# Squared deviation from the row mean: small leading loads folded into two large loads on one DMA queue

## The chip, the cores and the metric

The kernel runs on one core of one Trainium2 chip. The metric is the device time in microseconds (us); lower is better. The six executions of the kernel before agree within 0.16% (82.86 to 82.99 us). All differences in this study are below 3%, most below 0.5%, so they are read only against runs of the kernel before on the same chip.

A word used throughout: a *packet* is one contiguous run that one of the core's 16 DMA engines moves. Here it is one partition's part of one transfer, so a transfer over 128 partitions gives each engine 8 packets. The trace records the start, duration and size of each packet; where I quote these, the figures stand in plain fences or in the text, because the views of the profile only show them summed up. The record of a packet does not name its engine. I sorted the packets into 16 lines by letting each start where another had ended; for the large packets this is clear, for the small ones only sums and means over all 16 engines are safe.

## The reference

```python
batch, dim = 1024, 4096            # x: float32, axis = -1
mean = np.mean(x, axis=axis, keepdims=True)
return ((x - mean) ** 2).astype(np.float32)
```

16.78 MB are read and 16.78 MB written; there is next to no arithmetic per byte.

## The kernel before

Each of two tiles holds 4 rows on each of 128 partitions, so one partition's part of a tile is 64 KiB, contiguous in memory. Both tiles stay in on-chip memory, and all loads are issued at the start:

```python
for i in range(ntiles):                       # ntiles = 2, Q = 4, D = 4096, HEAD = 512
    x_tile = io.tile([P, Q * D], F32)
    if i == 0:
        nc.sync.dma_start(out=x_tile[:, :HEAD], in_=x_t[i][:, :HEAD])
        nc.sync.dma_start(out=x_tile[:, HEAD:], in_=x_t[i][:, HEAD:])
    else:
        end = Q * D - HEAD
        nc.scalar.dma_start(out=x_tile[:, end:], in_=x_t[i][:, end:])
        nc.sync.dma_start(out=x_tile[:, :end], in_=x_t[i][:, :end])
    ...
```

Per row, VectorE sums it (`pairs`, `neg_mean`) and ScalarE squares with the negative mean as bias. The last eighth of the last row is squared on VectorE. After its four rows a tile is stored in one transfer of 64 KiB runs from SP's queue.

## Time and profile before

| | before |
|---|---|
| median time | 82.99 us (82.96 to 82.99, 3 runs) |
| span in the profile | 81.4 us |
| DMA queues, share of 16 engines' span | 95.0% + 1.1% |
| VectorE, ScalarE busy | 26%, 36% |
| first packet starts, last packet ends | 1.75 us, 80.23 us |

The DMA engines work from 1.75 to 80.23 us, first loads, then stores, with no pause but 0.10 us on average at the turn between the two; compute lies beneath. The end is set by the engine that finishes last (80.23 us, and 1.13 more to the end of the span). The lines that show this are in the prediction. One more, in the windows cut at the stage borders, shows the start (the last two columns are DMA share and GB/s; a packet is credited to the window in which it starts, hence shares over 1):

```profile
1.70:4.10 2.40, 0.00 (x0) 0.00 (x0) 0.00 (x0) 1.00 1.76 642
```

In this window lie the 256 small packets of 2 KiB and the first large packet of each engine.

### The profile page before, as it was taken

The page shows a single profiled execution, that of the slowest core. Times are in us where ns is not written, and L with a number is a line of the kernel's source. Part 1 is how long each engine was busy: PE and PEld are TensorE (multiplying, and loading weights), DVE is VectorE, ACT ScalarE, POOL GpSimd, SP SyncE. Part 2 cuts the span into 40 slices and gives each one's busy share as a digit, 9 for nine tenths or more (in the row PEclk, how much of TensorE's full clock was granted, in tenths as well). Part 3 has the DMA queues.
Part 4 walks back from the last instruction along what each step waited for, and adds up shares of the span by engine and source line. Part 5 has one row for each costly group of instructions (what it writes and reads, how often), then busy time and mean ns, then how long its engine had stood idle before and what let it go on. Part 6 is the DMA issues. An engine that isn't in the chain of part 4 may idle for free.

```text
span 81.4 us, 87 instructions
## 1 busy us (share of the span) xinstructions
DVE 20.8 (26%) x20; ACT 29.4 (36%) x9; POOL 0.2 (0%) x4
## 2 busy tenths in 40 slices
DVE  0000000000059999600039999700000000000000
ACT  0000000000054999999502999999600000000000
POOL 0000000000000000000000000000000000000000
DMA  1974999999759999995799993899996599999390
GB/s 22 704 343 187 499 499 499 499 499 437 343 218 499 499 499 499 499 406 250 343 516 515 515 515 161 354 515 515 515 516 290 258 483 515 515 515 419 161 451 0
DMA packets 864, 33.55 MB, mean 412 GB/s; under 512 B 96, under 2 KB 96, under 8 KB 352
## 3 DMA queue, kind: packets, MB, share of 16 engines
q1 hardware_dynamic: 720, 33.29, 95.0%
q10 hardware_dynamic: 144, 0.26, 1.1%
HBM read 16.78 MB, written 16.78 MB: 412 GB/s over the span
## 4 chain that ended last, share of the span: by engine, by line
DMA 49%; ACT 13%; ACTq 4%; DVE 3%; SPq 1%; issue 0%
DMA x_tile<-in_x_dram 49%; ACT x_tile L77 13%; ACTq L119 4%; DVE pairs L66 3%; SPq L53 1%; SPq L52 0%; DVE neg_mean L66 0%
## 5 line engine op out<-in xcount | busy, mean ns | idle before, releaser
L77 ACT ACTIVATE x_tile<-x_tile,neg_mean 128x4096 f32<-128x4096 f32 (+1 forms) x8 | 28.2, 3590 | 5.7 <-DVE neg_mean L66 5.7
L66 DVE CUSTOM_DVE_ANT_0 pairs<-x_tile 128x2048 f32<-128x2048 f32 x8 | 18.3, 2292 | 31.6 <-DMA x_tile<-in_x_dram 31.4
L77 ACT ACT_TABLE_LOAD x1 | 1.3, 1283 | 23.2 <-DMA x_tile<-in_x_dram 23.2
L87 DVE TENSOR_TENSOR x_tile<-x_tile 128x512 f32<-128x512 f32 x2 | 1.4, 692 | 0.1
L86 DVE TENSOR_SCALAR x_tile<-x_tile,neg_mean 128x512 f32<-128x512 f32 x2 | 1.0, 488 | 0.1
L66 DVE DVE_READ_ACCUMULATOR2_ANT neg_mean<- 128x1 f32 x8 | 0.7, 82 | 0.0
L105 POOL MEMSET const-bfloat16-1.0<- 128x1 bf16 x1 | 0.1, 102 | 0.0
L105 POOL MEMSET const-uint8-127<- 128x1 uint8 x1 | 0.1, 102 | 0.0
L105 POOL MEMSET const-float32-0.0<- 128x1 f32 x1 | 0.1, 99 | 0.2 <-issue 0.2
L105 POOL MEMSET const-float32-1.0<- 128x1 f32 x1 | 0.1, 99 | 0.0
## 6 DMA issues: line engine op xcount, KB each, us to landing
x_tile<-in_x_dram SPq DMA_DIRECT2D x2, 7936.0 KB, 31.1
x_tile<-in_x_dram ACTq DMA_DIRECT2D x1, 256.0 KB, 3.8
x_tile<-in_x_dram SPq DMA_DIRECT2D x1, 256.0 KB, 3.6
out_dram<-x_tile SPq DMA_DIRECT2D x2, 21.9
```

Of the source, the lines that this page charges most:

```text
L53: nc.sync.dma_start(out=x_tile[:, HEAD:], in_=x_t[i][:, HEAD:])
L66: inorder(nc.vector.tensor_tensor_reduce(out=pairs, in0=row[:, :HALF], in1=row[:, HALF:], scale=-inv_d, scalar=0.0, op0=ADD, op1=ADD, accu ...
L77: nc.scalar.activation(out=row[:, :cut], in_=row[:, :cut], func=ACT.Square, bias=neg_mean, scale=1.0,)
L86: nc.vector.tensor_scalar_add(out=rest, in0=rest, scalar1=neg_mean)
L87: nc.vector.tensor_mul(out=rest, in0=rest, in1=rest)
L105: nc = _bacc.Bacc("TRN2", target_bir_lowering=False, num_devices=1)
L119: with _tile.TileContext(nc) as tc:
```

## The change

The intent: no small packets, no second queue, the longest runs throughout. Two loads and two stores, all with 64 KiB runs, all on SP's queue. Compute is untouched.

```diff
-    HEAD = 512
...
-        if i == 0:
-            nc.sync.dma_start(out=x_tile[:, :HEAD], in_=x_t[i][:, :HEAD])
-            nc.sync.dma_start(out=x_tile[:, HEAD:], in_=x_t[i][:, HEAD:])
-        else:
-            end = Q * D - HEAD
-            nc.scalar.dma_start(out=x_tile[:, end:], in_=x_t[i][:, end:])
-            nc.sync.dma_start(out=x_tile[:, :end], in_=x_t[i][:, :end])
+        nc.sync.dma_start(out=x_tile, in_=x_t[i])
```

## The prediction

The forecast's sum comes to 1.95 + 0.25 + 77.28 + 0.1 = 79.6 us for the last end, a gain of about 0.6, and 82.99 - 0.6 = 82.4 us. That run length is no lever rests on the two lengths shown, both at 434 GB/s.

> **What bounds the kernel now.** I read the page first, from its strip of 40 slices and its queue part.
>
> ```profile
> span 81.4 us, 87 instructions
> DMA  1974999999759999995799993899996599999390
> DMA packets 864, 33.55 MB, mean 412 GB/s; under 512 B 96, under 2 KB 96, under 8 KB 352
> q1 hardware_dynamic: 720, 33.29, 95.0%
> q10 hardware_dynamic: 144, 0.26, 1.1%
> ```
>
> The two queues together keep the 16 DMA engines busy for 95.0 + 1.1 = 96.1% of the span, while the page gives VectorE 26% and ScalarE 36%. The dips in the strip (4, 5, 3) are no idle time: a slice is 2.03 us and one large packet lasts longer than that, so a slice is credited with a packet or not. The windows cut at stage borders show it: from 4.1 to 22.8 us the DMA share is 1.00.
>
> ```profile
> 0.00:1.70 1.70, 0.00 (x0) 0.00 (x0) 0.20 (x4) 1.00 0.00 0
> 4.10:22.80 18.70, 0.00 (x0) 0.00 (x0) 0.00 (x0) 1.00 1.00 435
> 80.20:81.40 1.20, 0.00 (x0) 0.00 (x0) 0.00 (x0) 1.00 0.00 0
> ```
>
> The last two columns are DMA share and GB/s. Nothing moves before 1.7 us or after 80.2. The chain of waits, next, looks as if compute mattered:
>
> ```profile
> 1.64 40.26 DMA x_tile<-in_x_dram
> 41.92 2.29 DVE pairs L66
> 51.56 3.60 ACTq L119
> 55.16 3.17 ACT x_tile L77
> ```
>
> It stops at 55.16 + 3.17 = 58.33 us, when the last store is only being issued; the store that follows, some 22 us of it, is not in it. So I don't take its shares. The timeline and the table of DMA issues put the true order together:
>
> ```profile
> 0.73 0.39 ACTq L56 DMA_DIRECT2D x_tile<-in_x_dram  x1
> 0.73 0.38 SPq L52 DMA_DIRECT2D x_tile<-in_x_dram  x1
> 1.16 0.42 SPq L53 DMA_DIRECT2D x_tile<-in_x_dram  x1
> 23.29 2.29 DVE L66 CUSTOM_DVE_ANT_0 pairs<-x_tile 128x2048 f32<-128x2048 f32 x1 [23.29 <-DMA x_tile<-in_x_dram]
> 39.73 18.97 SPq L88 DMA_DIRECT2D out_dram<-x_tile  x2
> out_dram<-x_tile SPq DMA_DIRECT2D x2, 21.9
> ```
>
> The first store is issued at 39.73, the second at about 58.4. The packet records of the trace give the rest. One packet is one partition's run, and an engine carries 8 partitions of each transfer. A load packet of 63,488 B takes 2.342 us, with the next one starting 2.339 us after it; a store packet of 65,536 B takes 2.418 us, at a pitch of 2.415. The loads of tile 1 finish at 40.9 to 41.5 us and the store's packets start at 40.93 to 41.50 on the same engines, with a gap on two engines only (0.28 and 0.29 us). Store 0 then runs into store 1 without a hole, as store 1 is issued at 58.4 and store 0's last packets end at 60.2 to 60.9. Thus a DMA engine's line is unbroken from its first packet to its last, and compute lies under it. The kernel's time is: lead 1.75, small packets until the first large load packet (3.47 to 4.07, by engine), 16 load packets x 2.339 = 37.4, 16 store packets x 2.415 = 38.6, end at 79.57 to 80.23, and 1.13 of closing to 81.37. The measured 82.99 is 1.62 over that span; I take that as a constant.
>
> [...]16 x 65,536 B / 2.415 us = 434 GB/s for the stores and 16 x 63,488 B / 2.339 us = 434 for the loads, so [...]run length is no lever on the large packets. [...]the small packets of the ACT queue run from 1.92 to 4.07 us in between those of SP's (1.75 to 3.90), and the first large packet on an engine waits for both. [...]the two small loads are 256 KiB each, [...]16 small packets per engine cost 1.87 us where the bytes at the large packets' rate are 16 x 2,048 B / (65,536 B / 2.415 us) = 1.21.[...]
>
> **The change, part by part.** Removed: the two small loads (2 x 128 packets of 2 KiB, 2 x 16 completion packets), one issue on SP and one on ACT. The 4 KiB per partition go into the two large loads, whose packets grow from 63,488 to 65,536 B. Compute, stores and buffers stay; in the order of instructions nothing moves on VectorE or ScalarE.
>
> Bytes first: they are the same, so the 1.21 us per engine just computed stays. It comes back as 16 load packets x (2.415 - 2.339) = 1.21. What can go is the excess of the small packets, 1.87 - 1.21 = 0.66 us per engine. It has two parts. Of the 256 small packets 223 take 85 ns on average, 9 more than 2,048 B at the full rate (76): 16 x 9 = 0.15 us per engine. The other 33, about two per engine, are slow, 332 ns on average, 0.25 over the rest: 2 x 0.25 = 0.5 us per engine. They are mostly the first of their queue on an engine, so I read them as a start-up cost. The 0.15 goes for certain. Of the 0.5, one start-up may remain, because the first 64 KiB packet of an engine is now the first packet of all: 0.25. Sum: gain 0.66 at most, 0.41 with one start-up kept.
>
> Second, the spread. The engine that ends last sets the time. Before, the small packets scatter the first large ones over 0.60 us, and the last end (80.23) lies 0.3 after the mean end (79.92, mean of the 16). The first packets themselves started within about 0.2 us. If the engines now start within 0.2 and stay so, the last lies about 0.1 to 0.15 after the mean: gain about 0.15 to 0.2.
>
> The other way, added up: first packets at 1.75 to 1.95, one start-up of 0.25, 32 x 2.415 = 77.28, 0.1 at the turn from load to store, gives a last end of about 79.6, against 80.23: gain 0.65. Both ways agree on 0.5 to 0.8; I take 0.6. Time: 82.99 - 0.6 = 82.4 us, ratio 0.993.
>
> What is hidden: tile 0 is whole after 8 packets instead of the small ones and 8, so its landing moves from 23.2 to about 1.95 + 0.25 + 8 x 2.415 + 0.5 (last packet to VectorE, as before: 22.78 to 23.29) = 22.0. The compute of a tile takes 39.73 - 23.29 = 16.4 us, so store 0 is issued at about 38.4 rather than 39.73. Loads keep the engines until about 40.9, so those 1.3 us buy only the two short gaps at the turn. The ACT issue of 0.39 us is at a time when ScalarE waits for data until 23.24: worth nothing. Tile 1 lands at about 41.3, its compute ends at about 57.8, before store 0 is through at about 60.3.
>
> **The rivals.** *Start-up cost moves over whole:* the first 64 KiB packets each pay what the small ones paid, 0.5 us. For it: the slow packets may be slow because they are first at the memory, not because they are small.[...] Then 82.99 - 0.15 - 0.1 = 82.7. *Loads in step run slower:* all engines now read at nearly the same offset of rows 128 KiB apart, where before they were up to 0.6 us apart. If load packets took 5% longer, 38.6 x 0.05 = 1.9 us: 84.3 us, within 2%, just. Against it: two lanes of before that start within 0.001 us of each other show the same 2.342 us as all others, and the stores in the same layout run at 434 GB/s. *The early landing counts:* whoever trusts the chain of waits takes the 1.3 us off the end: 81.7. Against it: the engines have no hole to close. *A hole at the turn:* if compute were later than reckoned, store 0 would start late; the margin is about 2.5 us between issue and the end of the loads, and before it was 1.2 and already nearly enough.
>
> **Range and chances.** The floor is 32 x 2.415 = 77.28 plus lead 1.75, closing 1.13 and 1.62 outside the span: 81.8. Two per cent faster is 81.33, below this floor, so "faster" needs packets quicker than any seen: 0.02. "Slower" needs over 84.65, a load slowdown of over 5%: 0.03. The middle is 82.4; the floor plus some spread gives 82.0 as the low end, the moved start-up and a little loss gives 82.9 as the high end.
>
> **What would show it right or wrong.** Right: 576 packets on one queue (4 x 128 + 4 x 16), none between 512 B and 8 KB; load packets at 2.415 us; first packets at 1.75 to 1.95; VectorE starts at about 22.0, store 0 is issued at about 38.4, and no hole in the DMA line; last end about 79.6, span about 80.8. Wrong: a load packet over 2.45 us on average (the step that run length is no lever), a first packet longer by more than 0.5 us or a later first packet (start-up), a spread of last ends over 0.6 us, or VectorE's earlier start carried through to the end.

## The result and the profile after

The changed kernel took 83.32 us (median of 6 runs, 83.25 to 83.38) against 82.97 us before (6 runs, 82.86 to 82.99). The ratio is 1.0047, 95% interval 1.0034 to 1.0059: within 2%, but slower, where 82.4 had been forecast. Ratios here are the mean time of one kernel's fast runs over that of the other's fast runs of the same rounds, so they are not quite the ratio of the medians quoted.

The page of the changed kernel, first its strip and queue lines:

```profile
span 81.5 us, 81 instructions
DMA  9299975999984999987899998399998689999830
DMA packets 576, 33.55 MB, mean 412 GB/s; under 512 B 64, under 2 KB 64, under 8 KB 64
q1 hardware_dynamic: 576, 33.55, 95.8%
```

There are 576 packets on one queue, and the only ones under 8 KB are 64 of 4 B, 16 for each of the four transfers, which the prediction calls completion packets (96 before, for six transfers). But the engines are busy for 95.8% of the span, hardly less than the 96.1% of before, though 352 - 64 = 288 small packets are gone. So something else takes their time. The windows, same cuts as before:

```profile
1.70:4.10 2.40, 0.00 (x0) 0.00 (x0) 0.00 (x0) 1.00 1.30 437
4.10:22.80 18.70, 0.00 (x0) 0.00 (x0) 0.00 (x0) 1.00 1.04 449
80.20:81.40 1.20, 0.00 (x0) 0.00 (x0) 0.00 (x0) 1.00 0.00 0
```

The first window shows it. Its 437 GB/s over 2.4 us is one packet of 64 KiB per engine, 16 x 65,536 B / 2.4 us. At the full rate such packets take 16 x 2.418 us = 38.7 us of engine time, which is 38.7 / (16 x 2.4) = 1.01 of the window. The view has 1.30. The first packets take 1.3 times as long as they should. (The second window holds 128 packet starts, 8 rounds, hence a share a little over 1.) The packet records, sorted by start, say so one by one:

```
changed kernel, first 64 KiB packet of each engine (steady duration: 2.418 us)
start us  1.74 1.74 1.76 1.76 1.77 1.80 1.81 1.85 1.86 1.89 1.91 1.98 2.00 2.32 2.34 2.38
took us   3.11 2.96 3.21 3.05 3.07 3.16 3.12 3.09 3.45 3.11 3.10 3.35 3.54 2.57 2.98 2.93
```

On average a first packet takes 3.11 us, which is 0.69 over the steady duration. The other 496 packets of the kernel, loads and stores, are clean: none takes over 2.44 us. In the kernel before no large packet was over 2.364 us at the start, and the small ones had carried an excess of 0.66 us per engine.

Now the ends. A DMA engine's end is its first start, its first packet, and 31 packets at a pitch of 2.415 us:

| mean or extreme over the 16 engines, us | before | after |
|---|---|---|
| mean last end | 79.96 | 79.91 |
| latest last end | 80.23 | 80.39 |
| latest minus mean | 0.28 | 0.48 |
| span | 81.37 | 81.54 |

For after, the mean is 1.93 + 3.11 + 31 x 2.415 = 79.91, as recorded. The latest engine started at 2.00 and took 3.536 for its first packet: 2.00 + 3.54 + 74.87 = 80.41, recorded 80.39. So on average the engines end only 0.04 us sooner than before, and the last of them ends 0.16 us later, because the start-up is now paid in one lump per engine that varies from 0.15 to 1.12 us.

The small gain of the mean does not come from the start: the loads end at 41.27 us on average, 0.15 later than before (41.12), and on the last engine at 41.75, 0.25 later (41.50). It comes from behind them. The 0.10 us at the turn is gone, as store 0 was issued earlier, and the stores ran at 2.415 us per packet rather than 2.421, 0.10 over 16 packets. The pause before had a good side: it was paid mostly by the engines that were early, so it cut the distance from mean to last from 0.38 to 0.28.
The spans differ by 0.17. The two profiled executions took 83.14 and 83.32 us, a difference of 0.18; the other 0.17 of the 0.35 between the medians is that the profiled execution of before was slower than its median. No profile of a faster one was at hand.

The timeline after answers to the lines shown of before:

```profile
0.73 0.86 SPq L48 DMA_DIRECT2D x_tile<-in_x_dram  x2
22.81 2.29 DVE L57 CUSTOM_DVE_ANT_0 pairs<-x_tile 128x2048 f32<-128x2048 f32 x1 [22.81 <-DMA x_tile<-in_x_dram]
39.25 19.66 SPq L79 DMA_DIRECT2D out_dram<-x_tile  x2
out_dram<-x_tile SPq DMA_DIRECT2D x2, 22.2
```

VectorE starts at 22.81 rather than 23.29, store 0 is issued at 39.25 rather than 39.73, and little comes of it: the engines had only the 0.10 us at the turn to close, and the store waits in the queue a little longer. (The last line is from the table of DMA issues.)

### The profile page after: what moved, and what is told of

Read it like the earlier page. It is cut to its first block, busy times and chain, and to the rows that moved or that the text cites. A ratio compares the mean times of both kernels' runs of the same rounds, so it can differ in the third digit from the quotient of the medians.

```text
span 81.5 us, 81 instructions
## 1 busy us (share of the span) xinstructions
DVE 20.8 (25%) x20; ACT 29.4 (36%) x9; POOL 0.2 (0%) x4
## 3 DMA queue, kind: packets, MB, share of 16 engines
q1 hardware_dynamic: 576, 33.55, 95.8%
## 4 chain that ended last, share of the span: by engine, by line
DMA 50%; ACT 13%; ACTq 4%; DVE 3%; SPq 0%; issue 0%
DMA x_tile<-in_x_dram 50%; ACT x_tile L68 13%; ACTq L110 4%; DVE pairs L57 3%; SPq L48 0%; DVE neg_mean L57 0%
```

## The experiments

Three theories were put against each other at first. *A:* each DMA engine pays about 0.6 to 0.7 us once at its start, in whatever packets come first, and the scatter of this decides the end. *B:* large packets at the start cost more than small ones do. *C:* the issue of the second load, from about 1.2 to 1.6 us, disturbs the first packets. "Excess" below is what packets took over the steady duration of their size in the same trace, summed per engine and averaged over 16 engines. Diffs are against the changed kernel unless said otherwise. The costs per byte and per packet in the expectations are estimates from the traces of the two kernels: 27.1 B per ns is 65,536 B / 2.418 us, and 0.009 us per packet is what a packet of 2 KiB took over its bytes at that rate (85 against 76 ns).

### e1_head: the small head load alone

```diff
+        if i == 0:
+            nc.sync.dma_start(out=x_tile[:, :512], in_=x_t[i][:, :512])
+            nc.sync.dma_start(out=x_tile[:, 512:], in_=x_t[i][:, 512:])
+        else:
+            nc.sync.dma_start(out=x_tile, in_=x_t[i])
```

> The small head load of tile 0 (512 columns, SP) is put back, the ACT tail load is not. Theory A (start-up: each DMA engine pays about 0.6 us once at its start, in whatever packet comes first; the end is set by how far this start scatters the engines): the 8 small packets carry the start-up, their sum is about 1.2 us per engine, no large packet is over 2.45 us, mean last end about 79.8 to 79.9 us; the time lies between the two kernels, 82.9 to 83.2, by the scatter. Theory B (a large first packet pays more at start than small ones do, so small packets in front are a gain in themselves): large packets all at 2.42, time at or below the kernel before, 82.6 to 82.9. Theory C (issuing the second large load disturbs the first packets): second large load is issued at the same time as before, so first large packets would stay clean; no forecast of its own.

83.55 us (7 runs, 83.19 to 84.50) against 83.10; ratio of fast runs 1.0045 (1.0023 to 1.0066). The expectation of clean large packets failed: the small packets had an excess of 0.22 us, and the first large ones had 0.38 more. The sum, 0.60, fits theory A: eight packets of 2 KiB discharge a part of the start-up, not all of it. The profiled execution was a slow one (84.50 us: two engines had load packets of 3.0 and 3.3 us at 39.4 and 39.6 us), so its ends are not compared. Theory B is not borne out: a small load in front was no gain.

### e2_tail: the small ACT load alone

```diff
+        if i == 0:
+            nc.sync.dma_start(out=x_tile, in_=x_t[i])
+        else:
+            end = Q * D - 512
+            nc.scalar.dma_start(out=x_tile[:, end:], in_=x_t[i][:, end:])
+            nc.sync.dma_start(out=x_tile[:, :end], in_=x_t[i][:, :end])
```

> The ACT tail load of tile 1 (last 512 columns) is put back, the head load is not; the first packet on SP's queue is a 64 KiB one. Theory A: on each engine either the small ACT packet or the 64 KiB packet comes first; the first 64 KiB packet takes 2.6 to 3.5 us again, the time is that of the changed kernel, 83.2 to 83.4. Theory B: the same, 83.2 to 83.5, as the large packet is still the first on SP's queue, with 8 small ACT packets in between costing up to 0.15 us more. If it is instead the second queue that made the kernel before quick, the time is 82.9 to 83.0.

83.30 us against 83.10, ratio 1.0030 (1.0018 to 1.0042). On every engine a 64 KiB packet came first, with an excess of 0.67 us on average; the first small ACT packet started only at 4.76 us. As expected by A and B. A second queue that came behind a large packet changed nothing here.

### e3_warm: a tiny throw-away load in front

```diff
+        if i == 0:
+            warm = scratch.tile([P, 128], F32)
+            nc.sync.dma_start(out=warm, in_=x_t[i][:, :128])
         nc.sync.dma_start(out=x_tile, in_=x_t[i])
```

> The changed kernel with a throw-away load of 128 columns (512 B per partition, 64 KiB in all) into a spare tile ahead of the two 64 KiB-run loads. Pure additional bytes cost 8 x 512 B / 27.1 B per ns = 0.15 us per engine. Theory A: the 8 tiny packets carry the start-up, the 64 KiB packets are all 2.418 us, the mean last end moves by 0 to +0.2 against the changed kernel (79.9 to 80.1), time 83.2 to 83.5 unless the scatter shrinks. Theory B: the large packets no longer pay their large start-up, time falls to 82.7 to 83.1 although more bytes move. A third outcome, first 64 KiB packet still over 2.6 us, would say that the start-up belongs to large packets and not to an engine's first work.

84.06 us against 83.10, ratio 1.0120 (1.0105 to 1.0135): worse than any outcome listed. The third outcome came: the 512 B packets took about 27 ns each and showed no start-up, and the first large packets still had an excess of 0.47 us. On top, the engines had run out of tiny packets at 2.1 us, while the large load, issued 0.42 us later than in the changed kernel, brought first packets only at 2.24 to 3.12 us. Fourteen load packets around the issue of store 0 (39.50 us) took 2.48 to 3.00 us as well, 0.18 us per engine.

```profile
0.72 0.38 SPq L50 DMA_DIRECT2D warm<-in_x_dram  x1
1.15 0.90 SPq L51 DMA_DIRECT2D x_tile<-in_x_dram  x2
```

So eight packets of 512 B per engine in front did not clear the start-up.

### e4_late2: the second load issued late

```diff
+        if i == 1:
+            nc.vector.memset(x_tile[:, :2 * D], 0.0)
         nc.sync.dma_start(out=x_tile, in_=x_t[i])
```

> The changed kernel with the second load held back some 9 us by a VectorE memset of half of its tile[...]. It is issued well before the first load ends, so the DMA line stays whole. Theory C[...]: first packets fall to about 2.5 us and start within 0.2 us, last end about 79.5, time 82.7 to 83.0. Theories A and B: first packets 2.6 to 3.5 us as in the changed kernel, time 83.2 to 83.4.

83.38 us against 83.10, ratio 1.0039 (1.0021 to 1.0057). The second load was issued at about 9.3 us, long after the first packets were through, and the excess was 0.75 us, latest end 0.53 us after the mean. One load packet, at 39.2 us, took 2.62. Theory C falls.

### e5_hole: a second start from standing

```diff
+        if i == 1:
+            nc.vector.memset(x_tile, 0.0)
+            nc.vector.memset(x_tile, 0.0)
         nc.sync.dma_start(out=x_tile, in_=x_t[i])
```

> The changed kernel with the second load held back to about 30 us by two VectorE memsets of its whole tile, so that the DMA engines stand idle from about 22 to 31 us and start a second time (compute of tile 0 is late too; the time, about 92 us, is of no interest). If the start-up is paid whenever engines that stand idle start together, the first packet of the second load takes 2.6 to 3.5 us like that of the first, some 0.7 us over 2.418 on average. If it is paid once in an execution (first touch of the memory or of the queue), the second load's first packets take 2.42 us.

The windows of this run, cut at the first start, the hole, the second start and the steady part (columns: stretch, length, busy time and count of VectorE, ScalarE and GpSimd, clock, DMA share, GB/s):

```profile
1.70:4.70 3.00, 0.49 (x1) 0.00 (x0) 0.00 (x0) 1.00 1.02 350
22.60:36.00 13.40, 13.40 (x2) 1.24 (x1) 0.00 (x0) 1.00 0.00 0
36.00:39.00 3.00, 2.96 (x3) 1.70 (x1) 0.00 (x0) 1.00 1.06 350
39.50:50.00 10.50, 5.88 (x8) 10.50 (x4) 0.00 (x0) 1.00 1.01 437
```

The engines stood from 22.6 to 36 us. In the first 3 us after each start they moved one packet each (350 GB/s x 3 us / 16 = 65.6 KB) at a share of 1.02 and 1.06, where 2.418 / 3 = 0.81 would do. The packet records: 3.06 us on average at the first start, 3.18 at the second (2.72 to 3.45). The start-up is paid at every start from standing, not once in an execution. Each engine's last load packet was slow too, by 1.03 us on average; see e7.

### e6_pitch: another layout of rows

```diff
-    x_t = x.rearrange("(p n q) d -> n p (q d)", p=P, q=Q)
-    out_t = out.rearrange("(p n q) d -> n p (q d)", p=P, q=Q)
+    x_t = x.rearrange("(n p q) d -> n p (q d)", p=P, q=Q)
+    out_t = out.rearrange("(n p q) d -> n p (q d)", p=P, q=Q)
```

> The changed kernel with rows given to partitions tile by tile, so that a tile's 64 KiB runs follow one another in memory without gaps (pitch of 64 KiB rather than 128). If the start-up comes from the 16 engines meeting in the same places of memory at the start, it changes with the pitch: first packets 2.42 to 2.7, or far over 3.5. If not, first packets 2.6 to 3.5, extra of about 0.7 us per engine, time 83.2 to 83.5 as in the changed kernel.

83.35 us against 83.16, ratio 1.0025 (1.0010 to 1.0040). First packets 2.75 to 3.71 us, excess 0.75. In this second layout the start-up is the same, so the rival of engines reading "in step" finds no support at the start either. Five load packets at 38.7 to 39.3 us took 2.50 to 2.62; store 0 was issued at 39.17.

### e7_32k: loads cut in two

```diff
+        half = Q * D // 2
+        nc.sync.dma_start(out=x_tile[:, :half], in_=x_t[i][:, :half])
+        nc.sync.dma_start(out=x_tile[:, half:], in_=x_t[i][:, half:])
```

> The changed kernel with each load cut in two of 32 KiB runs: twice the load packets. Theory A (start-up is a time per engine, not a share of the packet): the first packet takes its 1.21 us plus about 0.67 on average, not plus 0.35; the per-packet cost adds 16 x 0.009 = 0.15 us; mean last end 79.9 to 80.2, time 83.2 to 83.6. If the start-up is in proportion to the first packet's size, the extra is about 0.35 and the time 82.8 to 83.1.

The start went by theory A: the first packets of 32 KiB took 1.81 us on average, 0.59 over their steady 1.213 (0.61 with a few slow second packets), nearly as much in time as the 64 KiB packets had. But the time was 84.40 us against 83.16, ratio 1.0153 (1.0136 to 1.0170), 0.8 above the forecast. The loss sits elsewhere: each engine's last two load packets, from 38.6 us on, took 1.79 us instead of 1.21, together 1.14 us per engine. The timeline shows what was new at that time:

```profile
31.95 20.77 SPq L81 DMA_DIRECT2D out_dram<-x_tile  x2
```

As compute could start on the first half of tile 0, store 0 was issued at 31.95 us, some 9.3 us before the loads would have ended (41.2 us, their mean end less the 1.14). That led to e10 and e14.

### e8_sp4: the four loads of before, all on SP's queue

```diff
-        nc.sync.dma_start(out=x_tile, in_=x_t[i])
         tiles.append(x_tile)
+    end = Q * D - 512
+    nc.sync.dma_start(out=tiles[0][:, :512], in_=x_t[0][:, :512])
+    nc.sync.dma_start(out=tiles[1][:, end:], in_=x_t[1][:, end:])
+    nc.sync.dma_start(out=tiles[0][:, 512:], in_=x_t[0][:, 512:])
+    nc.sync.dma_start(out=tiles[1][:, :end], in_=x_t[1][:, :end])
```

> All four loads of the kernel before, but on SP's queue alone, both small ones first: 16 small packets per engine ahead of the large ones, one queue. If 16 small packets (some 1.9 us in which the start-up is spread over many packets[...]) is what makes the kernel before quick: sum of the small packets 1.8 to 1.9 us per engine, large packets clean, the large loads issued 0.05 us later than before, time 82.9 to 83.1. If the two queues matter (packets of two queues taken in turn): first large packets slow again as in the run with the head alone, time 83.2 to 83.6.

85.60 us against 83.16, ratio 1.0298 (1.0282 to 1.0313): the worst of all, beyond both outcomes. The small packets ended by 3.74 us, but the first large packets of four engines began only at 4.56, 5.16, 5.20 and 5.89 us, and large packets of the first two rounds were slow (excess 1.23 us at the start). The timeline has the large loads issued third and fourth:

```profile
1.62 0.42 SPq L52 DMA_DIRECT2D x_tile<-in_x_dram  x1
2.09 0.43 SPq L53 DMA_DIRECT2D x_tile<-in_x_dram  x1
42.29 18.97 SPq L83 DMA_DIRECT2D out_dram<-x_tile  x2
```

That is 0.46 us later than in the kernel before, which explains neither the 2 us gaps nor the second slow round. Why four loads in a row on one queue with two small ones in front start so badly stays open. Four loads in a row by themselves do not: e7 had them, with a common start.

### e9_both0: both small loads from the front of tile 0

```diff
+        if i == 0:
+            nc.scalar.dma_start(out=x_tile[:, 512:1024], in_=x_t[i][:, 512:1024])
+            nc.sync.dma_start(out=x_tile[:, :512], in_=x_t[i][:, :512])
+            nc.sync.dma_start(out=x_tile[:, 1024:], in_=x_t[i][:, 1024:])
+        else:
+            nc.sync.dma_start(out=x_tile, in_=x_t[i])
```

> Like the kernel before, two small loads from SP and ACT ahead of the large ones, but both are from the front of tile 0 (columns 0 to 511 and 512 to 1023); tile 1 is one load of 64 KiB runs. If 16 small packets from two queues at the start are what holds the engines together, wherever their data go: small packets 1.8 to 1.9 us per engine, no slow large packet at the start, last end 0.2 to 0.35 us after the mean, time that of the kernel before within 0.15 us. If the place of the small data in tile 1 matters: first large packets slow, +0.2 to +0.4 us.

83.22 us against 83.01, ratio 1.0026 (1.0011 to 1.0042). At the start it did what was hoped: small excess 0.33 us, large packets nearly clean (0.04), mean last end 79.76 us, the earliest. Yet the latest end was 80.43, 0.66 after the mean, since six load packets took 2.51 to 2.76 us, around the time at which store 0 was issued (39.11 us); the slowest of them was on the engine that was latest anyway.

### e10_cut1: only tile 1's load cut in two

```diff
+        if i == 0:
+            nc.sync.dma_start(out=x_tile, in_=x_t[i])
+        else:
+            half = Q * D // 2
+            nc.sync.dma_start(out=x_tile[:, :half], in_=x_t[i][:, :half])
+            nc.sync.dma_start(out=x_tile[:, half:], in_=x_t[i][:, half:])
```

> The changed kernel with tile 1's load alone cut in two of 32 KiB runs. In the run with all loads cut, the last two load packets of each engine took 1.79 us on average rather than 1.21, and the first store had been issued 8 us before the loads ended (31.95 us). Here tile 0 is one load, so the first store is issued at about 39.2. If an early issued store slows the last loads: the last 32 KiB packets stay near 1.21 us, time 83.2 to 83.5. If 32 KiB runs themselves do so at the turn: the last packets at 1.6 to 1.9 us again, time 84.0 to 84.4.

83.36 us against 83.01, ratio 1.0050 (1.0022 to 1.0078). With store 0 issued at 39.00 us, the last 32 KiB packets had an excess of 0.03 us per engine instead of 1.14. So run length alone was not the reason in e7. The early store is what is left, and e5, with a store 4.7 to 5.2 us early, agrees.

### e11_tiny and e12_wide: the dose of the small packets

Both are the kernel before with one number changed, `HEAD = 512` to `HEAD = 128` and to `HEAD = 2048`.

> The kernel before with its small loads cut to 128 columns (512 B runs). Small packets then fill only about 0.4 us per engine. Theory A with its extension (the small packets carry the start-up[...]): the engines now run out of small packets at about 2.3 us, wait, and the first large packets are slow again (mean extra 0.4 to 0.7 us); last end 80.4 to 81.2, time 83.3 to 84.1. If any small packet at the start is enough: time 82.9 to 83.1.

83.53 us against 83.01, ratio 1.0059 (1.0040 to 1.0078). The queues and the order of issue are those of before; only the small packets are of 512 B. They took 0.45 us per engine and showed no start-up, and the first large packets were slow again, by 0.61 us. So a second queue is not enough by itself. Whether it helps beside packets of 2 KiB is not shown: e1, with one queue, has half as many of them, and e8, which was to tell, broke down. The run agrees with e3: packets too tiny leave the start-up to the large ones.

> The kernel before with its small loads widened to 2048 columns (8 KiB runs, 5 us of them per engine in all). Theory A: the start-up is in the first few packets of 8 KiB, about 0.5 to 0.7 us per engine in sum over 0.31 us each; large packets clean; time 82.9 to 83.2. If the scatter of the last ends falls below that of the kernel before (0.28 us after the mean), the time is the best yet, 82.8. If smallness of the packets is what counts: scatter and time as in the changed kernel, 83.3.

83.98 us against 83.01, ratio 1.0115 (1.0098 to 1.0131): missed. The start went as theory A said (excess of 0.42 us, all in the 8 KiB packets, large ones all at 2.116), but tile 1's 8 KiB packets ran beside tile 0's (the two small loads landed 7.3 and 7.1 us after their issue), tile 0 landed later (VectorE started at 24.89 us rather than 23.29) and with it the store came later:

```profile
41.33 17.17 SPq L88 DMA_DIRECT2D out_dram<-x_tile  x2
```

The loads ended at 40.93 to 41.26 us, the stores' first packets started at 42.17. All engines stood for about 1 us at the turn. A side effect is instructive: having waited for one common event, they ended within 0.16 us of each other (80.94 to 81.10). Scatter can be erased by a common wait, at the price of the wait; the kernel before and e2 show a little of the same at the turn.

### e13_again: the changed kernel on another chip

No edit.

> The changed kernel unaltered, once more, on another chip with 5 rounds. The small loss is real if it repeats: ratio 1.002 to 1.005, time 83.2 to 83.4 with the kernel before at 82.9 to 83.1; first packets 2.5 to 3.6 us, mean extra 0.6 to 0.75, last end 0.4 to 0.55 us after the mean. If it was this one chip: ratio 0.998 to 1.001.

83.26 us (5 runs) against 83.23, ratio 1.0011 (0.9997 to 1.0024). The start-up repeated: the first packets took 2.90 to 3.37 us, excess 0.73. Mean last end 79.94, latest 80.31, 0.37 after the mean. Eight load packets at 38.5 to 39.0 us took 2.49 to 2.66, around the issue of store 0 (38.92). The loss did not repeat: on this chip the kernel before itself took 83.23 us rather than 82.97. So what is settled is that the gain of 0.6 us is not there; the cost was 0.5% on the first chip and not clear of zero on the second. Whether it is the chip that makes this difference is not shown.

### e14_late_store: e9 with the store issued later

```diff
-    LAST = D - D // 8
+    LAST = D
```

(against e9: ScalarE squares the whole last row, which puts off the store.)

> The variant with both small loads from the front of tile 0, with the last row of each tile squared whole on ScalarE (LAST = D), which puts the first store off by about 0.43 us, from 39.11 to about 39.5. In that variant the mean end was 79.76 us, the earliest of all, but the last engine ended 0.66 later, some engines having had load packets of 2.5 to 2.8 us just when the store was issued. If the issue that comes before the loads are through causes this: no load packet over 2.45 us after 36 us, last end 0.25 to 0.35 after the mean, time 82.8 to 83.0, equal to or below the kernel before. If not: slow packets again, time 83.1 to 83.4.

83.22 us against 83.23, ratio 1.0004 (0.9989 to 1.0019). Store 0 was issued at 39.71 us, and no load packet after 36 us was over 2.45 us; the latest end was 0.34 after the mean. This is what was expected if the early store slows the loads, with one profile on each side and on two chips. The time was not below the kernel before, because the start-up was larger in this run (0.53 us against 0.33 in e9) and the mean last end was 79.89.

### e15_probe and e16_probe2: whose delay is it?

```diff
+    inorder = tc.keep_in_program_order
...
+        if i == 0:
+            inorder(nc.sync.dma_start(out=x_tile[0:2, :], in_=x_t[i][0:2, :]))
+            inorder(nc.sync.dma_start(out=x_tile[0:16, :], in_=x_t[i][0:16, :]))
+        inorder(nc.sync.dma_start(out=x_tile, in_=x_t[i]))
```

> The changed kernel with two loads ahead of tile 0's, each of 64 KiB runs into the same tile and so waited for: one of 2 partitions, then one of 16 partitions, then all 128. Each starts from standing engines. If the start-up is each engine's own delay: the first packets take about 3.1 us in all three. If it comes from 16 engines starting together: the 2 packets of the first load take 2.42 to 2.65 us, the 16 of the second 2.6 to 3.5, the first 16 of the third the same. If it belongs to several packets waiting in an engine's queue: 2.42 to 2.65 in the first two and 2.6 to 3.5 in the third alone. The time, about 90 us, is of no interest.

Inconclusive, and the probe's own fault. The two packets took 3.7 and 4.7 us and the sixteen 7.7 to 9.3 us: 1 MiB in 9.54 us, 110 GB/s. That is a quarter of the 434 GB/s of steady loads over 128 partitions, so the packets to partitions 0 to 15 were slow for more than the start-up; what slowed them is not shown. The third start of the run, on all 16 engines, had first packets of 2.87 to 3.51 us as usual. The second probe takes partitions that lie further apart, 64 and 4:

```diff
+            inorder(nc.sync.dma_start(out=x_tile[0:128:64, :], in_=x_t[i][0:128:64, :]))
+            inorder(nc.sync.dma_start(out=x_tile[0:32:4, :], in_=x_t[i][0:32:4, :]))
```

> The changed kernel with two loads ahead of tile 0's: one of partitions 0 and 64, then one of partitions 0, 4, ... 28, each of one 64 KiB packet per engine, each waited for; then all 128. Own delay of an engine: first packets of about 3.1 us in all three starts. Start together of 16: 2.42 to 2.65 us with 2 engines, 2.5 to 2.9 with 8, 2.6 to 3.5 with 16. If several packets waiting in an engine's queue are needed: 2.42 to 2.65 with 2 and with 8, 2.6 to 3.5 only in the third. The time, about 92 us, is of no interest.

The timeline has the three starts, each load waiting for the one before:

```profile
0.73 0.65 SPq L50 DMA_DIRECT2D x_tile<-in_x_dram  x1
6.16 0.67 SPq L51 DMA_DIRECT2D x_tile<-in_x_dram  x1
11.43 0.83 SPq L52 DMA_DIRECT2D x_tile<-in_x_dram  x2
```

```
first packets, us
 2 engines: 3.39 3.64
 8 engines: 2.89 3.36 3.36 3.28 3.28 2.89 3.03, and 2.42 on one that started 1.0 us after the rest
16 engines: 3.07 to 3.43
```

Two engines alone, each with a single packet, pay as much as sixteen together with eight packets each. No packet at these three starts took over 3.64 us. The start-up is each engine's own delay. It is not crowding, and not the length of the queue. The one late starter of the eight ended 0.1 us after the last of the others: the delay can show as a late start instead of a long packet, as it does for the three engines of the changed kernel that started at 2.32 to 2.38 us.

### All runs side by side

| run | median us | before, same chip | ratio | excess at the start, us | mean / latest last end, us |
|---|---|---|---|---|---|
| kernel before (profiled 83.14) | 82.97 | | | 0.52 + 0.15* | 79.96 / 80.23 |
| changed kernel | 83.32 | 82.97 | 1.0047 | 0.69 | 79.91 / 80.39 |
| e1_head | 83.55 | 83.10 | 1.0045 | 0.60 (slow run) | |
| e2_tail | 83.30 | 83.10 | 1.0030 | 0.67 | 80.15 / 80.34 |
| e3_warm | 84.06 | 83.10 | 1.0120 | 0.47 | 80.56 / 81.25 |
| e4_late2 | 83.38 | 83.10 | 1.0039 | 0.75 | 79.95 / 80.47 |
| e6_pitch | 83.35 | 83.16 | 1.0025 | 0.75 | 80.02 / 80.51 |
| e7_32k | 84.40 | 83.16 | 1.0153 | 0.61 | 81.04 / 81.28 |
| e8_sp4 | 85.60 | 83.16 | 1.0298 | 1.23 | 82.08 / 82.68 |
| e9_both0 | 83.22 | 83.01 | 1.0026 | 0.37 | 79.76 / 80.43 |
| e10_cut1 | 83.36 | 83.01 | 1.0050 | 0.63 | 79.96 / 80.41 |
| e11_tiny | 83.53 | 83.01 | 1.0059 | 0.61 | 80.22 / 80.59 |
| e12_wide | 83.98 | 83.01 | 1.0115 | 0.42 | 81.01 / 81.10 |
| e13_again | 83.26 | 83.23 | 1.0011 | 0.73 | 79.94 / 80.31 |
| e14_late_store | 83.22 | 83.23 | 1.0004 | 0.53 | 79.89 / 80.23 |

\* 0.15 is what 16 packets of 2 KiB cost over their bytes at the full rate in the steady state. e5 and the two probes were single looks with a hole made on purpose (99.51, 100.98 and 93.83 us). The same cost comes on top in e9 and e14 (0.15), e8 (0.15) and e1 (half of it). In e1, e3, e8 and e11 other things come in, as said there. Late first packets are not counted in the excess. No variant was faster than the kernel before.

## Why the prediction was wrong

**The bound was right.** After the change the engines work without a hole, large packets move at the same rate before and after (63,488 B in 2.342 us, 65,536 B in 2.418), and the bytes of the small packets came back as longer large ones. Compute, the ACT issue and the earlier landing were hidden, as said; the count of 576 packets on one queue was right.

**The step that failed first: "Of the 0.5, one start-up may remain, because the first 64 KiB packet of an engine is now the first packet of all: 0.25."** I had read the 33 slow small packets as two start-ups of 0.25 us per engine, one for each queue, of which one would go with its queue. The runs show one start-up per engine and start from standing, and not one per queue. Where a large packet came first it was 0.6 to 0.8 us on average, for packets of 64 and of 32 KiB, on one queue or two (changed kernel, e2, e4 to e7, e10, e13, e16). Where packets of 2 or 8 KiB came first on two queues it was 0.37 to 0.53 (e9, e12, before, e14), so it is not one constant either. In the kernel before it lay in the small packets (0.52 us of excess, and 0.15 of cost per packet besides), in the changed one in the first large packet (0.69). The term that was to go, 0.66, was replaced by 0.69. This was the first rival, "start-up cost moves over whole"; its mechanism was right, its size was put at 0.5. I had set it aside with an argument that no trace showed. The prediction's own sign of being wrong, "a first packet longer by more than 0.5 us", is what came.

**The step that failed second: the spread, "the last lies about 0.1 to 0.15 after the mean".** It was 0.48 us in the first profile and 0.37 on the other chip, against 0.28 before. I had argued from the starts of the first packets (0.2 us apart) and treated the start-up as the same for all engines. It ran from 0.15 to 1.12 us, and an engine that starts unlucky stays behind for all of its 31 further packets: each of the 16 lines of the trace has the same 32. Of the 0.20 more, half was there when the loads ended (0.48 against 0.38); the other half is the pause at the turn, which had narrowed the spread before. One profile is a small sample of it: e2, with large packets first as well, had 0.19, after 0.15 us of such a pause.

**The two together give the miss.** For the last engine the prediction reckoned 1.95 + 0.25 + 77.28 + 0.1 = 79.6; it measured 2.00 + (2.418 + 1.12) + 74.87 = 80.4. Of the 0.8 us, 0.87 is the start-up of the unluckiest engine, less the 0.1 allowed for the turn. The forecasts of VectorE's start (22.0, measured 22.81) and of store 0 (38.4, measured 39.25) were too early by the same start-up. Expected 0.6 faster, measured 0.35 slower on the first chip and 0.03 on the second.

**A slip in the level.** I took 82.99 - 81.37 = 1.62 us as the time outside the span, mixing a median with the span of an execution that took 83.14. The constant in these two executions is 1.77 (83.14 - 81.37; after, 83.32 - 81.54 = 1.78). It does not touch the difference, but the "floor" of 81.8 was 0.15 too low. Two readings were off as well: the mean last end before was 79.96, not 79.92, and the turn from load to store was not free on all engines but two. The gaps sum to 1.6 us over the 16, which is the 0.1 per engine that the sum allows; after the change they were gone.

**The rivals.** "Loads in step run slower" is refuted for this kernel: no load packet of it after the first took over 2.44 us. The slow ones of e6 and e13 lie around the issue of the store. "The early landing counts" is refuted: of the 1.3 us expected 0.5 came, and with it went the 0.10 at the turn. A landing still earlier came with slower loads (e7). "A hole at the turn" did not come in the changed kernel; e12 shows what it would have cost.

**What stays open.** What the start-up of an engine consists of; why packets of 512 B do not discharge it while sixteen of 2 KiB do; what happens in e8; and how much the change costs on a chip not tried.

## What to carry to other kernels

This kernel is bound by DMA engines that hardly pause (busy for 96.1% of the span before, 95.8% after). Here runs of 64 KiB in place of 62 and a landing 0.5 us earlier did not make it faster. In such a kernel, count what each engine pays once per start, and look at the engine that ends last, not at the mean. Here the first packet began 1.0 us after the issue started (0.73 to 1.74 us), and an engine's first 64 KiB then took 0.64 to 0.80 us over the steady 2.418 on average of 16 engines, and 1.0 and 1.2 with two engines, at every start from standing (changed kernel, e5, e16). The slow packets at the start were a cost of starting, so folding them into a larger transfer moved it instead of removing it. Have a store issued a little before the loads run out. An issue 1.9 to 2.0 us before their mean end left no gap (e11, changed kernel), 1.4 to 1.5 us left one of 0.04 to 0.15 us (before, e14, e2), one after their end left over 1 us (e12). One several microseconds too early went with slower loads ahead of it on the same queue: about 4.7 to 5.2 us ahead of an engine's loads' end (e5), the last load packet took 1.03 us more; some 9.3 us ahead (e7), the last two took 1.14 more together. Issued 1.1 to 1.9 us ahead, it slowed no load in the kernel before and in e14. Between 1.9 and 2.5 us, single packets took up to 0.6 us more in some runs (e3, e6, e9, e13) and none did in the changed kernel. What the engines do in that time is not shown.
